# S5 recurrence as one chain per layer in a hybrid S5, RetNet and Hyena step

## The chip, the cores and the metric

The kernel runs on one core of one Trainium2 chip. The metric is the device time of one launch in microseconds; before the change it was 1736.06 us (median of three runs, 1731.86 to 1738.31). Five engines run side by side: PE multiplies matrices into PSUM, DVE, ACT and POOL work on elements, and SP issues most of the DMAs. Each engine takes its instructions in the order in which the program puts them.

## The reference

A trunk of four layers works on 128 context tokens and 256 latent tokens, 384 in all, with 1024 features. Layers 0 and 3 are bidirectional S5 layers, layer 1 is retention, layer 2 Hyena. An S5 layer projects its input to `u` and a gate, and drives one complex diagonal state of 64 dimensions for each of 64 groups of 16 features, in both directions:

```python
_, _, h_re, h_im = lax.associative_scan(combine, (a_re, a_im, bu_re, bu_im), axis=1)
y = (jnp.einsum('blgp,ghp->blgh', h_re, c_re) - jnp.einsum('blgp,ghp->blgh', h_im, c_im))
# in s5_branch, with y summed over both directions and the skip:
g = jax.nn.gelu(y)
y = g * jax.nn.sigmoid(g @ w_glu + b_glu)
out = (y * jax.nn.silu(gate)) @ w_out
```

The context starts from a zero state and returns its final states; the latent tokens start from states that are given (`h0`).

## The kernel before

Tokens are cut into chunks of eight: 16 chunks of context and 32 of latent tokens, 48 columns of states in all. Everything that can be done for all chunks at once is a matrix product; only the step from one chunk's state to the next is a recurrence, on DVE.

One S5 layer (`s5`, from line 692) runs in stages. The P stage follows a plan, a string of letters (`PLAN0` for layer 0, `PLAN1` for layer 3, lines 76 and 77). `U n` projects two blocks of features and sends them through DRAM into the layout `U` (`u_epi`, line 756). `A n` makes or loads the matrices PB up to number n; in layer 0 they are computed on DVE, POOL and PE (`gen_b1`, `gen_b2`), in layer 3 loaded. `P n` (`use_p`, line 733) multiplies them with `U`, transposes the product on PE, and ACT copies it into the states X (line 752). `T` runs a piece of background work, the modulation vectors of later layers (`mod_unit`, line 367). `R q` runs the recurrence of one half of the groups (`recur`, line 764): `R0` stands behind `P3`, `R1` at the plan's end.

X is held in two tiles (`Xs`, `NH = 2` halves of 32 groups). A tile has, for two directions and 32 groups, 49 places of one word each, so the neighbouring groups of one chunk lie 49 words apart. `recur` advances two chains, latent (31 steps) and context (16 steps), and each takes both directions in one instruction: 2 x 32 = 64 columns on 128 partitions. A step is five DVE instructions, lines 786 to 790: a shuffle that swaps real and imaginary lanes, X times A1, its addition to the next place, the shuffled state times A2, its addition. The context's last step goes into XF, which an ACT queue stores as the final states. The scratch tiles `sw` and `m1` are in the pool `tmp`, two buffers each.

Behind the plan comes the gate: `dense` (line 830) multiplies four slabs of weights of the input projection, eight units of 24 products, into PSUM tiles of the pool `pd`, which has three buffers. Each weight unit is split into a high and a low part (`unit`, line 156), the high on ACT, the low by a subtraction that in this stage is always POOL's (`sub_any`, line 144; `PSG = 3`); the split tiles have two buffers. `silu2` (line 529) ends a unit: tanh on ACT, then line 532 on DVE, which reads the PSUM tile and writes a block of `sgate`. `sgate` is the one tile of the pool `s5r`, [128, 8, 384] in f32.

The output stage (from line 854) is a loop over eight pairs of group blocks: line 874 multiplies U with a Toeplitz matrix, lines 875 and 876 add the states X times the matrices CP, forward and backward. Blocks 0 to 3 read the first half of X, 4 to 7 the second. In layer 0 some CP are computed on the way (`gen_c`, line 678): those of the first two blocks wholly on POOL (`CPG = 2`), others on DVE with one addition on POOL. GELU, the GLU projection and the output projection follow.

Pools are taken from a stack with a left and a right end and closed in the opposite order; those of `s5` have `reuse_waits="tile"`, so a tile waits for the users of earlier tiles on its own bytes. In a layer the left end holds, in this order, `s5h`, in layer 0 `s5t`, and then the P stage's pools: the ring of PB (`s5b`), `s5a` and in layer 0 `s5g`. They are closed at line 820, and `s5r` and `s5c` follow. The program's order on each engine is set by a scheduler that takes what stands earlier in the program first, among what it expects to be ready.

Of the kernel before, what the change touches and what calls it, by code (L numbers as in the profile page):

```python
# [10 lines left out]
F32 = mybir.dt.float32  # L11
# [15 lines left out]
NCH = T // Q  # L27
XP = NCH + 1
CC = NCTX // Q
# [4 lines left out]
SPLIT = True  # L34
RB = 7
NBC = 2
NH = 2
CPG = 2
RB1 = 10
CP1 = 6  # L40
# [32 lines left out]
GV = 7  # L73
LSQ = 0
FPB = (3, 6)
PLAN0 = "A7 U0 T1 U1 T1 P0 A9 T1 P1 A11 T1 U2 T1 P2 A13 T1 P3 A15 T1 R0 U3 T1 P4 T1 A16 P5 T1 T1 P6 P7 R1"
PLAN1 = "A10 U0 U1 P0 A12 P1 A13 U2 P2 A16 P3 R0 U3 P4 P5 P6 P7 R1"
SPL = (4, 6, 8, 10, 12, 14)
SPQ = "gpsimd"
KSE = "VG"  # L80
# [25 lines left out]
def hybrid_trunk(ctx: ExitStack, tc: tile.TileContext, I, O, dbg=None, layers=(0, 1, 2, 3)):  # L106
    nc = tc.nc
    V, S, G, TE = nc.vector, nc.scalar, nc.gpsimd, nc.tensor
# [5 lines left out]
    tmp = ctx.enter_context(tc.tile_pool(name="tmp", bufs=2))  # L114
# [577 lines left out]
    def s5(i, j, nxt, begun=lambda: None):  # L692
        def mk(st, name, bufs=1, **kw):
            return st.enter_context(tc.tile_pool(name=f"{name}_{i}", bufs=bufs, reuse_waits="tile", **kw))
# [3 lines left out]
        U = pool.tile([128, 8, 8 * NCH + 16], F32, name="U")  # L698
        XH = 64 // NH
        Xs = [pool.tile([128, 2 * XH, XP], F32, name=f"X{q}") for q in range(NH)]  # L700
        XFs = [pool.tile([128, 2, XH], F32, name=f"XF{q}") for q in range(NH)]
        hpool = mk(ep, "s5h")
# [13 lines left out]
                gates.popleft()()  # L716
        V.memset(U[:, :, 8 * NCH:], 0.0)
        eP = ExitStack()
        ring = mk(eP, "s5b", RB if j == 0 else RB1)
        ru = mk(eP, "s5a", 2)  # L720
        PBs = {}
# [42 lines left out]
        def recur(q):  # L764
            gs = slice(q * XH, (q + 1) * XH)
            A1, A2 = Av[:, 0, :, gs], Av[:, 1, :, gs]
            X, XF = Xs[q], XFs[q]
            Xb = X[:, 0, 0:1]
            V.tensor_copy(XF[:, 0], X[:, 0:XH, CC])
            V.tensor_copy(XF[:, 1], X[:, XH:2 * XH, 0])  # L770

            def view(c_f, c_b):
                return bass.AP(tensor=Xb.tensor, offset=Xb.offset + c_f,
                               ap=[Xb.ap[0], [XH * XP + c_b - c_f, 2], [XP, XH]])
            V.memset(view(0, CC), 0.0)
            V.tensor_copy(view(CC, NCH), h0.rearrange("p (d g) -> p d g", d=2)[:, :, gs])
            for k in range(NCH - CC - 1):
                for c0, n in ((CC, NCH - CC), (0, CC)):
                    if k >= n:
                        continue  # L780
                    c1 = c0 + n - 1
                    cur = view(c0 + k, c1 - k + 1)
                    dst = XF if k == n - 1 else view(c0 + k + 1, c1 - k)
                    sw = tmp.tile([128, 2, XH], F32, tag=f"sw{c0}{q}", name="sw")
                    m1 = tmp.tile([128, 2, XH], F32, tag=f"m1{c0}{q}", name="m1")
                    V.stream_shuffle(sw, cur, [(x + 16) % 32 for x in range(32)])  # L786
                    V.tensor_mul(m1, cur, A1)  # L787
                    V.tensor_add(dst, dst, m1)  # L788
                    V.tensor_mul(sw, sw, A2)  # L789
                    V.tensor_add(dst, dst, sw)  # L790
            nc.scalar.dma_start(O["ns5"][j].rearrange("p (d g) -> p d g", d=2)[:, :, gs], XF)

        nxp = 0
# [1 line left out]
        def ahead(n):  # L795
            nonlocal nxp
            while nxp < min(n, 16):
                get_p(nxp)
                nxp += 1
        if j == 0 and AI:  # L800
            with tc.issue_after(ADA[0]):
                ahead(AI)
        for op in (PLAN0, PLAN1)[j].split():
            n = int(op[1:])
            if op[0] == "A":
                ahead(n)
            elif op[0] == "U":
                if j == 0:
                    pool_share[0] = PS0 if n == 0 else 1
                firstmajor(i, weight(I["s5_w_in"][j, n]), h, u_epi, 2 * n)  # L810
                if n == 0:
                    begun()
            elif op[0] == "P":
                use_p(n)
            elif op[0] == "R":
                recur(n)
            else:
                tick(n)
        pool_share[0] = PSG
        eP.close()  # L820
        if j == 0:
            eT.close()
        rpool = mk(ep, "s5r")
        sgate = rpool.tile([128, NB, T], F32, name="sgate")

# [560 lines left out]
    def to3():  # L1386
        p = pool_of(e3, "x3", side="right")
        return Early(3, lambda: p.tile([128, T + 2], F32, tag="xb", name="xb", bufs=NB + EB3))
    s5(0, 0, to1)
    trace(0)  # L1390
    hp = pool_of(eh, "hp")
# [5 lines left out]
    e2.close()  # L1397
    eh.close()
    s5(3, 1, lambda: None, e3.close)
    trace(3)  # L1400
    rb, _ = rstd_bcast()
# [168 lines left out]
```

## Time and profile before

| | us |
|---|---|
| median of three runs | 1736.06 |
| lowest and highest run | 1731.86, 1738.31 |
| span of the profiled execution | 1732.9 |
| PE busy in it | 1576.3 (91%) |
| DVE busy in it | 1331.7 (77%) |
| POOL busy in it | 762.2 (44%) |
| ACT busy in it | 691.6 (40%) |

Layer 0 takes about the first 450 us of the span and layer 3 the last 300. The rows further down give the start of an instruction from the span's start, its duration in us, the engine, the line, what is written and read with shapes, and in brackets how long the engine was idle just before and what ended that. A group by line has a count, the busy time and the mean in ns. A row of a stretch has, for each engine, the busy time with the number of instructions, then the granted clock of PE (1.00 is its full level) and what the DMA engines did.

### The profile page before, as it was taken

To read this page: it belongs to the slowest core of one execution; us is meant where nothing else is said; L and a number is where in the kernel's file an instruction comes from. 1 tells how busy PE (TensorE), PEld (TensorE's weight loads), DVE (VectorE), ACT (ScalarE), POOL (GpSimd) and SP (SyncE) were. 2 spreads that over 40 slices of the span, in tenths; PEclk is the share of its full clock that TensorE was granted. 3 is DMA by queue.
4 is the path that set the end of the run, shared out by engine and by line. 5 is a ranking of instruction groups with operands and counts; after the bars stand their busy time and mean duration, and the time that the engine had idled before them with its cause. 6 is when DMAs were issued, how large, how long until landed. Compare 5 with 4: busy or idle time off the path is not lost. (4 is left out here: it accounts for less than half of the span.)

```text
span 1732.9 us, 27790 instructions
## 1 busy us (share of the span) xinstructions
PE 1576.3 (91%) x10370; PEld 1348.6 (78%) x10370; DVE 1331.7 (77%) x3064; ACT 691.6 (40%) x1275; POOL 762.2 (44%) x542
## 2 busy tenths in 40 slices
PE   5899856898899999999899999999999999986996
PEld 3565545787588888899879889888898797775996
DVE  8979999889886777747767788687687864399355
ACT  2434320343333343335354444454454543521343
POOL 2767352525274757532235545555566231230221
PEclk9799978999799999999989999999999999987998
DMA  8356655644655656543421222222222363755431
GB/s 339 110 184 221 185 124 151 211 178 146 219 163 169 203 183 211 180 137 129 142 87 65 95 95 74 95 71 73 95 89 74 122 240 114 212 166 174 132 121 62
DMA packets 103199, 253.02 MB, mean 146 GB/s; under 512 B 28023, under 2 KB 68056, under 8 KB 83480
## 3 DMA queue, kind: packets, MB, share of 16 engines
q1 hardware_dynamic: 80768, 200.12, 35.5%
q0 software_dynamic: 7376, 26.48, 4.5%
q10 hardware_dynamic: 14920, 24.65, 3.9%
q8 instruction: 82, 1.34, 0.3%
q14 instruction: 53, 0.43, 0.1%
HBM read 220.37 MB, written 30.83 MB: 145 GB/s over the span
## 5 line engine op out<-in xcount | busy, mean ns | idle before, releaser
L134 POOL TENSOR_TENSOR wl<-wr,wh 128x1024 fp32r<-128x1024 f32 (+2 forms) x101 | 248.9, 2465 | 342.6 <-ACT wh L162 320.1
L139 PE MATMUL psd<-hh,wh 128*128 128x384 f32 x880 | 308.8, 352 | 38.2 <-DVE sgate L532 33.2
L162 ACT CAST wh<-wr 128x1024 fp32r<-128x1024 f32 (+4 forms) x211 | 215.9, 1029 | 316.7 <-PE psd L139 221.2
L139 PE MATMUL psd<-hh,wl 128*128 128x384 f32 x880 | 308.0, 351 | 3.9 <-DVE wl L149 2.0
L139 PE MATMUL psd<-hl,wh 128*128 128x384 f32 x880 | 307.7, 350 | 0.4 <-DVE hl L470 0.2
L139 PEld LDWEIGHTS psd<-hh,wh 128*128 128x128 f32 x880 | 171.5, 195 | 49.3 <-issue 40.4
L149 DVE TENSOR_TENSOR wl<-wr,wh 128x1024 fp32r<-128x1024 f32 (+3 forms) x110 | 149.2, 1358 | 78.7 <-ACT wh L162 78.3
L139 PEld LDWEIGHTS psd<-hh,wl 128*128 128x128 f32 x880 | 170.6, 194 | 13.4 <-issue 6.4
L139 PEld LDWEIGHTS psd<-hl,wh 128*128 128x128 f32 x880 | 171.0, 194 | 10.2 <-issue 6.7
L134 POOL TENSOR_TENSOR BP<-BP,xt 128x512 f32<-128x512 f32 x64 | 97.6, 1528 | 82.3 <-DVE xt L630 49.2
L134 POOL TENSOR_TENSOR CP<-CP,xt 128x512 f32<-128x512 f32 x64 | 94.9, 1487 | 85.6 <-DVE xt L630 66.8
L139 PE MATMUL psd<-wh,hh 128*128 128x256 f32 x384 | 110.4, 292 | 1.5 <-ACT k L1070 1.5
L139 PE MATMUL psd<-wl,hh 128*128 128x256 f32 x384 | 110.0, 288 | 1.2 <-DVE wl L149 1.2
L139 PE MATMUL psd<-wh,hl 128*128 128x256 f32 x384 | 108.7, 285 | 0.0
L664 PE MATMUL psm<-BP,bc 128*32 128x128 f32 x512 | 76.0, 296 | 7.0 <-POOL BP L134 6.3
L139 PE MATMUL psd<-zb,wh 128*128 128x384 f32 x240 | 80.9, 338 | 0.0
L630 DVE TENSOR_TENSOR xt<-FI,bc 128x512 f32<-128x512 f32 x64 | 64.0, 1008 | 16.7 <-POOL BP L134 11.8
L139 PEld LDWEIGHTS psd<-wh,hh 128*128 128x128 f32 x384 | 73.8, 194 | 2.7 <-ACT k L1070 1.9
L139 PEld LDWEIGHTS psd<-wl,hh 128*128 128x128 f32 x384 | 74.3, 193 | 1.9 <-DVE wl L149 1.4
L139 PEld LDWEIGHTS psd<-wh,hl 128*128 128x128 f32 x384 | 74.3, 194 | 0.3 <-issue 0.2
L665 PE MATMUL psm<-ident,BP 128*128 128x128 f32 x256 | 69.7, 325 | 3.4 <-DVE kk L1013 2.0
L629 DVE TENSOR_TENSOR BP<-F,bc 128x512 f32<-128x512 f32 x64 | 57.9, 914 | 17.8 <-PE psm L665 15.5
(387 smaller groups left out, 4095.0 us busy)
## 6 DMA issues: line engine op xcount, KB each, us to landing
wr<-in_mod_w_dram SPq DMA_DIRECT2D x40, 1024.0 KB
wr<-in_hy_w_in_dram SPq DMA_DIRECT2D x32, 1024.0 KB
wr<-in_ret_w_in_dram SPq DMA_DIRECT2D x24, 1024.0 KB
wr<-in_s_w_in_dram SPq DMA_DIRECT2D x16, 1024.0 KB
wm<-in_mod_w_dram SPq DMA_DIRECT2D x8, 1024.0 KB
Tt<-scratch_kd_dram SPq DMA_DIRECT2D x128, 64.0 KB
wr<-in_s_w_glu_dram SPq DMA_DIRECT2D x8, 1024.0 KB
wr<-in_s_w_out_dram SPq DMA_DIRECT2D x8, 1024.0 KB
```

What stands on the lines that cost most here:

```text
L134: G.tensor_tensor(out, a, b, op=op)
L139: TE.matmul(out, lhs[a], rhs[b], start=start and i == 0, stop=stop and i == len(combos) - 1)
L149: V.tensor_sub(out, a, b)
L162: S.copy(hi, ap)
L629: eng.tensor_tensor(out, c1, x[:, 0].unsqueeze(2).to_broadcast([128, 4, 8, 16]), op=OP.mult)
L630: eng.tensor_tensor(t, c2, x[:, 1].unsqueeze(2).to_broadcast([128, 4, 8, 16]), op=OP.mult)
L664: TE.matmul(psk[32 * g:32 * g + 32, d * 128:(d + 1) * 128], xcf[:, g * 16:g * 16 + 32], bp, start=True, stop=True)
L665: TE.transpose(ps[:, g * 128:(g + 1) * 128], bp, ident)
```

## The change

The recurrence is run once a layer. `NH` becomes 1, so X is one tile of 64 groups, and the two halves' chains become one with 2 x 64 = 128 columns. The context no longer has steps of its own: it starts eight steps later (`LAG = 8`), and for 15 steps an access pattern with one more dimension takes the latent and the context place in the same instruction, 256 columns (`pair`); the last context step, into XF, stays alone. `R0` stands at the plan's end, behind `P7`, in both plans, and `R1` is gone. The scratch tiles `sw` and `m1` move from `tmp` to a pool of their own, `s5rr`, with one buffer each; it is opened ahead of the ring and closed behind it, before `s5r` is opened.

```diff
-NH = 2
+NH = 1
+LAG = 8
-PLAN0 = "A7 U0 T1 U1 T1 P0 A9 T1 P1 A11 T1 U2 T1 P2 A13 T1 P3 A15 T1 R0 U3 T1 P4 T1 A16 P5 T1 T1 P6 P7 R1"
-PLAN1 = "A10 U0 U1 P0 A12 P1 A13 U2 P2 A16 P3 R0 U3 P4 P5 P6 P7 R1"
+PLAN0 = "A7 U0 T1 U1 T1 P0 A9 T1 P1 A11 T1 U2 T1 P2 A13 T1 P3 A15 T1 U3 T1 P4 T1 A16 P5 T1 T1 P6 P7 R0"
+PLAN1 = "A10 U0 U1 P0 A12 P1 A13 U2 P2 A16 P3 U3 P4 P5 P6 P7 R0"
...
         eP = ExitStack()
+        eR = ExitStack()
+        rr = mk(eR, "s5rr")
         ring = mk(eP, "s5b", RB if j == 0 else RB1)
...
+            swap = [(x + 16) % 32 for x in range(32)]
+
+            def step(cur, dst, a1, a2, shape):
+                sw, m1 = (rr.tile(shape, F32, tag=f"{nm}{len(shape)}", name=nm) for nm in ("sw", "m1"))
+                V.stream_shuffle(sw, cur, swap)
+                V.tensor_mul(m1, cur, a1)
+                V.tensor_add(dst, dst, m1)
+                V.tensor_mul(sw, sw, a2)
+                V.tensor_add(dst, dst, sw)
+
+            def pair(k, s):
+                f, b = k - LAG + s, CC - (k - LAG) - s
+                return bass.AP(tensor=Xb.tensor, offset=Xb.offset + f,
+                               ap=[Xb.ap[0], [XH * XP + b - f, 2], [CC + LAG, 2], [XP, XH]])
+            wide = [a.unsqueeze(2).to_broadcast([128, 2, 2, XH]) for a in (A1, A2)]
             for k in range(NCH - CC - 1):
-                for c0, n in ((CC, NCH - CC), (0, CC)):
-                    if k >= n:
-                        continue
-                    c1 = c0 + n - 1
-                    cur = view(c0 + k, c1 - k + 1)
-                    dst = XF if k == n - 1 else view(c0 + k + 1, c1 - k)
-                    sw = tmp.tile([128, 2, XH], F32, tag=f"sw{c0}{q}", name="sw")
-                    m1 = tmp.tile([128, 2, XH], F32, tag=f"m1{c0}{q}", name="m1")
-                    V.stream_shuffle(sw, cur, [(x + 16) % 32 for x in range(32)])
-                    V.tensor_mul(m1, cur, A1)
-                    V.tensor_add(dst, dst, m1)
-                    V.tensor_mul(sw, sw, A2)
-                    V.tensor_add(dst, dst, sw)
+                if LAG <= k < LAG + CC - 1:
+                    step(pair(k, 0), pair(k, 1), *wide, [128, 2, 2, XH])
+                    continue
+                step(view(CC + k, NCH - k), view(CC + k + 1, NCH - k - 1), A1, A2, [128, 2, XH])
+                if k == LAG + CC - 1:
+                    step(view(CC - 1, 1), XF, A1, A2, [128, 2, XH])
...
         eP.close()
         if j == 0:
             eT.close()
+        eR.close()
```

## Rows read from the trace of the kernel before

**Rows 1.** Busy time by stretch: around the recurrence of layers 3 and 0.
```profile
1526.00:1594.00 68.00, 46.81 (x268) 40.61 (x266) 68.00 (x380) 13.37 (x23) 14.81 (x7) 0.80 0.59 170
...
202.00:250.00 48.00, 33.82 (x204) 29.88 (x203) 48.00 (x216) 11.08 (x19) 20.72 (x14) 0.86 0.50 135
250.00:272.00 22.00, 1.40 (x4) 0.80 (x4) 22.00 (x37) 1.33 (x2) 20.46 (x16) 0.56 0.26 58
```
**Rows 2.** Timeline of PE in layer 3's gate stage: first products of units.
```profile
1525.09 0.33 PE L139 MATMUL psd<-hh,wh 128*128 128x384 f32 x1
...
1529.25 0.33 PE L139 MATMUL psd<-hh,wh 128*128 128x384 f32 x1
...
1534.10 0.66 PE L139 MATMUL psd<-hh,wh 128*128 128x384 f32 x1 [4.34 <-DVE sgate L532]
1534.56 0.52 PE L139 MATMUL psd<-hl,wh 128*128 128x384 f32 x1
...
1539.36 0.48 PE L139 MATMUL psd<-hl,wh 128*128 128x384 f32 x1
```
**Rows 3.** Timeline of PE: where line 875 waited for X, both layers.
```profile
288.51 0.42 PE L875 MATMUL psm<-CP,X 128*48 128x128 f32 x2 [2.93 <-DVE X L790]
...
325.12 0.66 PE L875 MATMUL psm<-CP,X 128*48 128x128 f32 x2 [3.38 <-DVE X L790]
...
1594.40 0.66 PE L875 MATMUL psm<-CP,X 128*48 128x128 f32 x2 [4.86 <-DVE X L790]
```
**Rows 4.** Timeline of DVE: two chains side by side, one shuffle and its next.
```profile
1523.10 0.26 DVE L786 STREAM_SHUFFLE sw<-X 128x64 f32<-128x64 f32 x1
...
1524.78 0.25 DVE L786 STREAM_SHUFFLE sw<-X 128x64 f32<-128x64 f32 x1
```
**Rows 5.** Timeline of DVE: one chain alone, a whole step.
```profile
1598.15 0.26 DVE L786 STREAM_SHUFFLE sw<-X 128x64 f32<-128x64 f32 x1
1598.33 0.25 DVE L787 TENSOR_TENSOR m<-X,A 128x64 f32<-128x64 f32 x1
1598.50 0.21 DVE L789 TENSOR_TENSOR sw<-sw,A 128x64 f32<-128x64 f32 x1
1598.63 0.26 DVE L788 TENSOR_TENSOR X<-X,m 128x64 f32<-128x64 f32 x1
1598.93 0.27 DVE L790 TENSOR_TENSOR X<-X,sw 128x64 f32<-128x64 f32 x1
...
1599.24 0.26 DVE L786 STREAM_SHUFFLE sw<-X 128x64 f32<-128x64 f32 x1
```
**Rows 6.** DVE's groups by line and shape, whole span: widths and a strided copy.
```profile
L320 DVE TENSOR_TENSOR vs<-vs 128x128 f32<-128x128 f32 x4 | 1.1, 283 | 0.0
...
L176 DVE TENSOR_TENSOR zl<-zz,zh 128x384 fp32r<-128x384 f32 x16 | 8.8, 552 | 3.0 <-ACT zh L175 2.9
...
L1068 DVE STREAM_SHUFFLE rsw<-psd 128x256 f32<-128x256 f32 x16 | 7.2, 450 | 0.0
...
L770 DVE COPY XF<-X 128x32 f32<-128x32 f32 x4 | 0.7, 181 | 0.0
```
**Rows 7.** Timeline of ACT: the last copies of P7 into X.
```profile
201.31 1.01 ACT L752 COPY X<-psm 128x384 f32<-128x384 f32 x2 [3.15 <-PE psm L749]
...
1523.85 1.00 ACT L752 COPY X<-psm 128x384 f32<-128x384 f32 x2 [3.41 <-PE psm L749]
```
**Rows 8.** DVE's groups from 202 to 288.4 us: the recurrence's two-input operations.
```profile
L789 DVE TENSOR_TENSOR sw<-sw,A 128x64 f32<-128x64 f32 x59 | 22.9, 388 | 0.0
L787 DVE TENSOR_TENSOR m<-X,A 128x64 f32<-128x64 f32 x57 | 22.3, 391 | 0.0
L788 DVE TENSOR_TENSOR X<-X,m 128x64 f32<-128x64 f32 x57 | 22.3, 391 | 0.0
L790 DVE TENSOR_TENSOR X<-X,sw 128x64 f32<-128x64 f32 x57 | 20.1, 409 | 0.0
```
**Rows 9.** POOL's groups from 1525.2 to 1594.4 us.
```profile
L134 POOL TENSOR_TENSOR wl<-wr,wh 128x1024 fp32r<-128x1024 f32 x6 | 14.6, 2432 | 23.8 <-ACT wh L162 23.7
```

## The prediction

> **What bounds the kernel now.** I read the busy time by stage first, then PE's timeline, then DVE's own timeline, and last what POOL does beside it. In the stage after the last state projection of layer 3, from 1526 to 1594 us, DVE is busy 68.00 us of 68.00 and PE 46.81 [rows 1]: the recurrence is the bound there. PE has only the gate projection left and stands behind DVE, since a PSUM tile of the gate comes free only when DVE has run line 532 on it: 4.34 us at 1534.10 [rows 2]. Then PE waits for X: line 875, the first product that reads the states, begins at 1594.40 in layer 3 and at 288.51 in layer 0, both released by line 790 [rows 3]. In layer 0 a second wait of 3.38 us stands at 325.12, for the second half of the groups [rows 3]. So in both layers the end of the recurrence sets when the output stage begins. Layer 0 is worse off: from 250 to 272 us PE works 1.40 us of 22 while POOL is busy 20.46 [rows 1].
>
> **What the change removes.** 47 steps by two halves and two layers are 188 steps, of five instructions each. Two chains side by side take 1.68 us for two steps, from shuffle to shuffle [rows 4], 0.84 each; 94 steps a layer are 79 us of DVE. Where one chain runs alone, a step takes 1.09 us, as 0.18 + 0.17 + 0.13 + 0.30 + 0.31 from start to start [rows 5]: the last two carry about 0.12 us more, because each needs the result of the instruction just ahead of it. The new recurrence is always one chain.
>
> **What it adds.** A layer has 16 + 1 steps on 128 columns and 15 on 256. A contiguous two-input operation takes 283 ns at 128 columns and 552 at 384, thus 1.05 ns a column [rows 6]; back to 64 that gives 216, what line 789 takes (0.21), and lines 787, 788 and 790, which read or write X at a stride of 49 words, take 0.25 to 0.27 [rows 5]. The excess of some 45 ns is either a price of each strided column, 0.7 ns, or a fee per instruction. I take the first: the 32-column copy out of X takes 181 ns [rows 6], where 216 less 32 columns (34) plus a fee of 45 would be 227 and the price by column 204. The trace has no wide strided operation, so this is a bound from both sides and not shown. [...] The shuffle grows from 0.26 us at 64 columns to 0.450 at 256 [rows 5, 6], 1.0 ns a column from a contiguous source; between that and 1.75 I take 1.4. So a step on 128 columns is 1.09 + 3 x 0.112 + 0.067 + 0.09 = 1.58 us and one on 256 is 1.09 + 3 x 0.336 + 0.202 + 0.27 = 2.57. 17 x 1.58 + 15 x 2.57 = 65.4 us a layer: a third of the instructions, but only 14 us less DVE time.
>
> **What it moves.** The first chain began after P3 and ran beside P4 to P7; now nothing begins until P7's copies into X end, at 202.32 in layer 0 and 1524.85 in layer 3 [rows 7]. The four set-up instructions cost about 0.6 us. DVE's work in the P stage goes away, but PE is full there, so I take no gain; at most 3 us. Of queues, only the store of XF on ACT moves; it leaves once, near the end, behind gate work that is then done.
>
> **POOL's holds.** Two-input DVE operations stand still while POOL runs one: between 202 and 288.4 us the four lines average 391, 391, 388 and 409 ns [rows 8] against 0.25, 0.26, 0.21 and 0.27 [rows 5], which is 8.0 + 7.5 + 10.5 + 7.9 = 34 us, 0.82 of the 41.2 us that POOL was busy from 202 to 272 [rows 1]. I price a hold at 0.82 of POOL's time; the ends are 0.6 (a wider operation gets more done between two holds) and 1.0.
>
> **The wait that it adds.** `s5rr` is opened ahead of the ring and closed behind it, and `s5r` is the next pool opened on that side. Pools are stacked, so `s5r` begins on the byte where `s5rr` began: `sgate`, 12 KB a partition, covers the 3 KB of `sw` and `m1`. With `reuse_waits="tile"` a tile waits for all users of earlier tiles on its bytes; here the last is the recurrence's last addition. Before, `sw` and `m1` lay in `tmp` and `sgate` stood on ring tiles, dead after P7. So every line 532 must follow the whole recurrence on DVE. Behind it are queued: three finished PSUM tiles of the gate, all that `pd` has, and thus PE's gate units 4 to 8. They had run beside the recurrence; now they run after it. One unit is 24 products from 1525.09 to 1529.25, 4.16 us at full clock [rows 2], five are 20.8. After that wait PE's products take 0.32 us each against 0.173, fifteen from 1534.56 to 1539.36, 2.4 us lost with the first two [rows 2]; the granted clock of the stretch is 0.80 [rows 1]. With 0.5 us for line 532 (552 ns at 384 columns, [rows 6]) PE reaches the output stage's work 23.7 us after the recurrence ends, whichever of the two it takes first.
>
> **Layer 3.** 1524.85 + 0.6 + 65.4. Of POOL's six subtractions in that stretch (2.43 us each, [rows 9]) only the splits of three units still find a buffer ahead of the end: 3 x 2.43 x 0.82 = 6.0. The recurrence ends at 1596.9, the output stage is at 1620.6 against 1594.40: 26 us later.
>
> **Layer 0.** POOL's 24 operations of `gen_c` stay beside the recurrence (41.2 less six subtractions of 2.4 leaves 27) with three subtractions, 34.2 x 0.82 = 28. 202.32 + 0.6 + 65.4 + 28 = 296.3, and with 23.7 it is 320.0 against 288.51, 31.5 later. The wait of 3.38 us at 325.12 goes, since all groups now end together: 28.
>
> **Sum.** 54 us on the span of 1732.9, that is 1787. The runs' median of 1736.06 is 3.2 above this execution's span, so I forecast 1790.
>
> **Rivals.**
> *The gate isn't held back*: `sgate` waits by the bytes really shared or lies elsewhere, and the eight line 532 slip into the chain's gaps. For it: I read the overlap from the code, and no row shows such a wait. Then 8 x 0.47 us join the recurrence, and all six subtractions: layer 3 ends at 1524.85 + 0.6 + 65.4 + 12.0 + 3.8 = 1606.7, 12 later; layer 0 at 202.32 + 0.6 + 65.4 + 34 + 3.8 = 306.1, 18 less 3.4 later. 1736 + 26 = 1762.
> *The stride is a fee per instruction*, the gate held: steps of 1.09 + 5 x 0.067 = 1.43 and 1.09 + 5 x 0.202 = 2.10 give 55.7 a layer, 19 less in all: 1771. The copy of 181 ns speaks against it.
> *Not slower: a step costs the same whatever its width*, as if only the count of instructions mattered. 32 x 1.09 = 35 us a layer, 30.5 less in each: layer 3 is 4 us ahead of before and layer 0 about 2.5, 1736 - 7 = 1729. It decides from about 35 us a layer, a mean of 0.22 us an instruction. The rows of 283 and 552 ns speak against it; what speaks for it is that no wide strided row exists.
>
> **How the numbers follow.** About half a per cent, 8.7 us, is what a measurement of this kernel can tell from no change: same is 1727.4 to 1744.7. The held gate 0.66, its own range 1772 to 1806 (holds at 0.6 or 1.0 of POOL's time are 15 us apart over both layers, the shuffle's slope 4, products of the gate that PE moves ahead a few). The gate not held 0.16, of which 0.03 below 1744.7. The fee 0.08. Flat steps 0.10, half of it below 1727.4. Slower 0.66 + 0.13 + 0.08 = 0.87, same 0.03 + 0.05 = 0.08, faster 0.05. From 1755 to 1806 lie nearly all of the held gate and the fee and most of the second case, about 0.8.
>
> **What would show it.** Right: lines 786 to 790 come 32 times a layer each; wide operations on X take 0.59 to 0.63 us (0.37 to 0.39 on 128 columns); no line 532 between the first and the last shuffle of a layer; PE idle for most of the recurrence and then five gate units before or among the output stage. Wrong: line 532 among the steps, 256-column operations of 0.45 us, a first line 875 ahead of 1594 us in layer 3, or a P stage that ends much earlier.

## The result and the profile after

The changed kernel takes 1791.7 us (median of four runs, 1788.35 to 1796.04) against 1737.0 for the kernel before beside it: a ratio of 1.0314, 95% interval 1.0289 to 1.0339. The forecast was 1790. The profiled execution has a span of 1788.8 us, 55.9 longer than the one before.

The page's head comes first, engine by engine (share of the span, instructions).

```profile
PE 1566.9 (88%) x10370; PEld 1343.1 (75%) x10370; DVE 1279.1 (72%) x2312; ACT 690.7 (39%) x1275; POOL 765.1 (43%) x542
```

DVE has 52.6 us less work than before (1331.7) and PE about the same, and yet the span is longer: PE waits more. The busy time by stretch tells where (layer 3's recurrence, the time just behind it, the later part of layer 0's recurrence; columns as in rows 1).

```profile
1551.00:1623.00 72.00, 14.18 (x79) 12.61 (x77) 69.68 (x188) 6.42 (x11) 7.84 (x4) 0.58 0.30 78
1625.00:1655.00 30.00, 30.00 (x197) 27.02 (x199) 3.34 (x7) 6.26 (x10) 8.30 (x5) 0.97 0.37 123
250.00:290.00 40.00, 0.00 (x0) 0.00 (x0) 38.96 (x104) 0.00 (x0) 4.71 (x4) 0.50 0.03 8
```

Before, PE was busy 46.81 us of 68 beside layer 3's recurrence [rows 1]; now it is 14.18 of 72 beside the recurrence and 30.00 of 30 behind it. From 250 to 290 us it does nothing at all, at a granted clock of 0.50. PE's timeline shows the waits that answer to rows 3, and what follows the second one.

```profile
291.34 0.63 PE L887 MATMUL psm<-CP,X 128*48 128x128 f32 x2 [58.67 <-DVE X L788]
...
1624.05 0.66 PE L887 MATMUL psm<-CP,X 128*48 128x128 f32 x2 [50.21 <-DVE X L788]
...
1628.01 0.44 PE L140 MATMUL psd<-hh,wh 128*128 128x384 f32 x1
```

One wait of 58.67 and one of 50.21 us have taken the place of 2.93, 3.38 and 4.86 [rows 3], and four microseconds after the second, line 140 is running: gate units, which before ran ahead of it [rows 2]. DVE's timeline has the reason: the first writes of `sgate` in layer 0, then the end of layer 3's recurrence with a step on 256 columns, a step on 128 and the first writes of `sgate` there.

```profile
291.23 1.48 DVE L533 SCALAR_TENSOR_TENSOR sgate<-silu,psd 128x384 f32<-128x384 f32 x3
...
1586.08 0.60 DVE L784 STREAM_SHUFFLE sw<-X 128x256 f32<-128x256 f32 x1
1586.59 0.59 DVE L785 TENSOR_TENSOR m<-X,A 128x256 f32<-128x256 f32 x1
1587.10 0.42 DVE L787 TENSOR_TENSOR sw<-sw,A 128x256 f32<-128x256 f32 x1
1587.43 0.61 DVE L786 TENSOR_TENSOR X<-X,m 128x256 f32<-128x256 f32 x1
1588.07 0.61 DVE L788 TENSOR_TENSOR X<-X,sw 128x256 f32<-128x256 f32 x1
...
1588.73 0.60 DVE L784 STREAM_SHUFFLE sw<-X 128x256 f32<-128x256 f32 x1
...
1615.95 0.38 DVE L784 STREAM_SHUFFLE sw<-X 128x128 f32<-128x128 f32 x1
1616.24 0.37 DVE L785 TENSOR_TENSOR m<-X,A 128x128 f32<-128x128 f32 x1
1616.53 0.28 DVE L787 TENSOR_TENSOR sw<-sw,A 128x128 f32<-128x128 f32 x1
1616.73 0.38 DVE L786 TENSOR_TENSOR X<-X,m 128x128 f32<-128x128 f32 x1
1617.14 0.39 DVE L788 TENSOR_TENSOR X<-X,sw 128x128 f32<-128x128 f32 x1
...
1617.57 0.38 DVE L784 STREAM_SHUFFLE sw<-X 128x128 f32<-128x128 f32 x1
...
1623.61 0.39 DVE L788 TENSOR_TENSOR X<-X,sw 128x128 f32<-128x128 f32 x1
1624.09 1.48 DVE L533 SCALAR_TENSOR_TENSOR sgate<-silu,psd 128x384 f32<-128x384 f32 x3
```

The first writes of `sgate` are three of line 533 in a row, in layer 3 0.1 us behind the last addition of the last step. In both layers none of the eight writes of `sgate` stands between the first and the last shuffle; in the kernel before all eight do. The three are the three full PSUM tiles that the prediction spoke of. A step from shuffle to shuffle takes 1.62 us on 128 columns and 2.65 on 256.

How the 55.9 us are spread is read from the start of the same instructions in both traces. Layer 1's first product of queries and keys comes at 493.1 and 523.3 us: up to there the change costs 30.2, which I count to layer 0. Layer 2's last product (line 497 here, 496 before) starts 25.8 later, so layers 1 and 2 give 4.4 back, and the last copy into X in layer 3 starts 24.7 later. Layer 3's first product with X is 29.6 later, its last 55.6, the end 55.9: layer 3 costs 30.1, of which its P stage (up to that copy) gives 1.1 back and the rest takes 31.2.

### The profile page after: what moved, and what is told of

Read it like the earlier page. It is cut to its first block, busy times and chain, and to the rows that moved or that the text cites. A ratio compares the mean times of both kernels' runs of the same rounds, so it can differ in the third digit from the quotient of the medians.

```text
span 1788.8 us, 27046 instructions
## 1 busy us (share of the span) xinstructions
PE 1566.9 (88%) x10370; PEld 1343.1 (75%) x10370; DVE 1279.1 (72%) x2312; ACT 690.7 (39%) x1275; POOL 765.1 (43%) x542
## 3 DMA queue, kind: packets, MB, share of 16 engines
q8 instruction: 82, 1.34, 0.3%
## 5 line engine op out<-in xcount | busy, mean ns | idle before, releaser
L140 PE MATMUL psd<-hl,wh 128*128 128x384 f32 x880 | 303.7, 345 | 4.5 <-DVE hl L471 4.4
L140 PE MATMUL psd<-hh,wh 128*128 128x384 f32 x880 | 303.8, 346 | 3.3 <-ACT wh L163 3.3
L140 PE MATMUL psd<-hh,wl 128*128 128x384 f32 x880 | 303.6, 346 | 0.7 <-DVE wl L150 0.7
L140 PEld LDWEIGHTS psd<-hh,wh 128*128 128x128 f32 x880 | 167.8, 191 | 13.5 <-issue 6.0
L887 PE MATMUL psm<-CP,X 128*48 128x128 f32 x256 | 50.7, 282 | 108.9 <-DVE X L788 108.9
L887 PEld LDWEIGHTS psm<-CP,X 128*48 128x48 f32 x256 | 30.1, 127 | 112.7 <-issue 62.0
```

The lines of the kernel that those rows point to most:

```text
L140: TE.matmul(out, lhs[a], rhs[b], start=start and i == 0, stop=stop and i == len(combos) - 1)
L887: TE.matmul(o48, Xs[gg // XH][:, gg % XH, 0:48], CP[r][:, 0, g].rearrange("p a b -> p (a b)"), start=False, stop=False)
```

## The experiments

All kernels beside each other, in the order of the text. "Chain" is the time from the start of the last copy into X (line 752 before) to the first product with X (line 875 before), "output" from there to the start of the last one (line 876 before), from the view of each line; both for layers 0 and 3. Ratios are to the kernel before on the same chip (medians from 1736.0 to 1737.3), with 95% intervals.

| kernel | us | ratio | chain 0 | output 0 | chain 3 | output 3 |
|---|---|---|---|---|---|---|
| before | 1737.0 | | 86.7 | 62.0 | 70.0 | 54.8 |
| after | 1791.7 | 1.0314 (1.0289 to 1.0339) | 95.6 | 83.7 | 74.9 | 80.8 |
| e1_free | 1755.2 | 1.011 (1.0075 to 1.0145) | 104.8 | 56.7 | 85.8 | 55.8 |
| e2_lock | 1778.9 | 1.0231 (1.0208 to 1.0255) | 76.6 | 92.6 | 59.7 | 87.2 |
| e3_halves | 1732.7 | 0.9968 (0.9953 to 0.9984) | 62.3 | 89.1 | 61.7 | 58.6 |
| e8_late | 1769.9 | 1.0187 (1.0163 to 1.0211) | 112.6 | 60.7 | 88.4 | 55.9 |
| e10_unmerged | 1770.7 | 1.0202 (1.0177 to 1.0227) | 111.7 | 58.0 | 91.4 | 56.2 |
| e4_contig | 1735.1 | 0.9982 (0.9967 to 0.9997) | 92.9 | 58.0 | 68.3 | 55.4 |
| e5_halves_contig | 1713.0 | 0.9867 (0.9848 to 0.9886) | 58.9 | 79.7 | 47.9 | 60.0 |
| e9_contig3 | 1715.1 | 0.9877 (0.9862 to 0.9892) | 60.3 | 89.1 | 48.0 | 55.1 |
| e6_nopool | 1778.9 | 1.0241 (1.0226 to 1.0257) | 79.0 | 84.3 | 74.9 | 81.7 |

### Is it the wait of `sgate`?

**e1_free**, the changed kernel without the overlap:

```diff
-        eR = ExitStack()
-        rr = mk(eR, "s5rr")
...
-                sw, m1 = (rr.tile(shape, F32, tag=f"{nm}{len(shape)}", name=nm) for nm in ("sw", "m1"))
+                sw, m1 = (tmp.tile(shape, F32, tag=f"{nm}{len(shape)}", name=nm, bufs=1) for nm in ("sw", "m1"))
...
-        eR.close()
```

> The changed kernel with one thing undone: the scratch tiles sw and m1 lie in the pool tmp again (one buffer each), so sgate shares no byte with them. Theory (the wait of sgate on the recurrence's scratch is what costs most): the eight lines that write sgate slip between the steps, the gate units of the matrix engine run beside the recurrence again, and the stage from the first product with X to the last falls from 80.8 us in layer 3 and 83.2 in layer 0 (changed kernel) to 55 to 60. The recurrence gets 8 x 0.47 us and three more subtractions of POOL, 3 x 2.43 x 0.82, thus about 10 us longer in each layer. 1791.7 - 2 x 25 + 2 x 10 = about 1762. Rival (one chain that is always ready keeps VectorE full, and the gate would come behind it in any case): no line that writes sgate among the steps, 1785 to 1795.

It took 1755.2 us, 36.5 less than the changed kernel. DVE's timeline in layer 3 has the writes of `sgate` among the steps again (this kernel's line numbers are two to three lower):

```profile
1536.35 0.29 DVE L785 TENSOR_TENSOR sw<-sw,A 128x128 f32<-128x128 f32 x1
1536.55 2.60 DVE L784 TENSOR_TENSOR X<-X,m 128x128 f32<-128x128 f32 x1
1538.99 0.54 DVE L533 SCALAR_TENSOR_TENSOR sgate<-silu,psd 128x384 f32<-128x384 f32 x1
1539.46 0.37 DVE L786 TENSOR_TENSOR X<-X,sw 128x128 f32<-128x128 f32 x1
```

Line 533 even falls into the gap between two dependent additions, and in both layers all eight writes of `sgate` stand among the steps. The output stages of layers 3 and 0 shrink to 55.8 and 56.7 us as the theory said, and the chains grow by 10.9 and 9.2. The rival, that a chain which is always ready would keep the gate behind it anyway, is out.

**e2_lock**, the kernel before with that overlap alone:

```diff
+        eR = ExitStack()
+        rr = mk(eR, "s5rr", 2)
         ring = mk(eP, "s5b", RB if j == 0 else RB1)
...
-                    sw = tmp.tile([128, 2, XH], F32, tag=f"sw{c0}{q}", name="sw")
-                    m1 = tmp.tile([128, 2, XH], F32, tag=f"m1{c0}{q}", name="m1")
+                    sw = rr.tile([128, 2, XH], F32, tag=f"sw{c0}{q}", name="sw")
+                    m1 = rr.tile([128, 2, XH], F32, tag=f"m1{c0}{q}", name="m1")
...
+        eR.close()
         rpool = mk(ep, "s5r")
```

> The kernel before with that wait alone: its scratch tiles (two buffers) in a pool that is opened ahead of the ring of PB and closed behind it, so that sgate falls on their bytes. Four chains, two halves, as before. Theory: all lines that write sgate come behind both halves' recurrence, and the matrix engine's gate units 4 to 8 (five x 4.16 us) with the half-clock ramp move behind it; since the first half of the output stage can start without the gate, part of the 27 us of that half covers the second half's recurrence: layer 0 about 17 us later, layer 3 about 15, 1737 + 32 = 1769 (1755 to 1784). Rival (the wait is harmless): 1737, or up to 10 less since the steps are no longer interrupted.

1778.9 us, 42 more than before, within the range but above the 32. DVE again ends the recurrence and then writes three tiles at once:

```profile
1619.45 0.27 DVE L792 TENSOR_TENSOR X<-X,sw 128x64 f32<-128x64 f32 x1
1619.82 1.49 DVE L532 SCALAR_TENSOR_TENSOR sgate<-silu,psd 128x384 f32<-128x384 f32 x3
```

So the wait alone costs 42 us in the kernel with four chains, and by e1 36.5 of the 55 in the changed one. I had let the second half's chain hide part of the gate units. The output stage of layer 3 is 32.4 us longer than before, though its chain is 10.3 shorter: PE is busy 83.33 of the 87.40 us from 1607.6 on, so the gate units had nothing to hide behind.

### Which part of the rest is the cost?

**e3_halves** keeps the merged step but in two halves, with the plans of before and the scratch of e1:

```diff
-NH = 1
+NH = 2
...
-PLAN1 = "A10 U0 U1 P0 A12 P1 A13 U2 P2 A16 P3 U3 P4 P5 P6 P7 R0"
+PLAN1 = "A10 U0 U1 P0 A12 P1 A13 U2 P2 A16 P3 R0 U3 P4 P5 P6 P7 R1"
```

> The merged step, but in two halves of 32 groups with the plans of before (R0 behind P3, R1 at the end), scratch in tmp. A half has 17 steps on 64 columns and 15 on 128. Theory (what the merged step loses is the gap of a lone chain, about 0.25 us a step, and the start behind P7; width costs by the column): the two halves fill each other's gaps, steps side by side cost 0.84 us at 64 columns and about 1.4 at 128, so 34 x 0.84 + 30 x 1.4 = 70.6 us a layer against 79 before, and the first half again starts in the P stage: 7 us less per layer than the kernel before, 1723 (1712 to 1737). Rival (merging gains nothing since the time is by the column alone): 1735 to 1742.

**e8_late** is e3 with the first half made to wait: in both plans `R0` stands beside `R1` behind `P7`, both halves' XF copies come first, and the start values of a half are `0 * XFs[1]`, plus `h0`, so they need P7. Of the edit, the start values:

```diff
...
-            V.memset(view(0, CC), 0.0)
-            V.tensor_copy(view(CC, NCH), h0.rearrange("p (d g) -> p d g", d=2)[:, :, gs])
+            V.tensor_scalar(view(0, CC), XFs[1], 0.0, None, op0=OP.mult)
+            V.scalar_tensor_tensor(view(CC, NCH), XFs[1], 0.0, h0.rearrange("p (d g) -> p d g", d=2)[:, :, gs],
+                                   op0=OP.mult, op1=OP.add)
```

> e3 with one thing undone: both halves start together behind the last copy into X, since the first half's start values are made from a tile that the last block fills (0 times it, added). Theory (the early start of the first half is worth its DVE time in the P stage, 8 x 1.09 + 5 x 1.58 = 16.6 us in layer 3, and the two halves then end together): from the last copy into X to the first product with X, layer 3 goes from 61.7 us to 80 to 86, about what the single chain of e1 took (85.8), and the time to 1748 to 1756. Rival (the start is of no worth, since the second half ends last in either case): 1730 to 1738.

e3 took 1732.7 us: faster than before, but by 4, not 14. Layer 3 gives what was expected, 7.4 us from layer 2's last product to the end (P stage 2.8 shorter, chain 61.7 against 70.0, output 3.8 longer). Layer 0 gives nothing: its chain is 24.4 us shorter and its output stage 27.1 longer, and layer 1's first product of queries and keys comes 7.8 later, of which layers 1 and 2 give 4.8 back. Before e3's first product with X in layer 3, PE waits 3.78 us. In e8, PE's timeline has 26.23:

```profile
1631.80 0.66 PE L886 MATMUL psm<-CP,X 128*48 128x128 f32 x2 [26.23 <-DVE X L788]
```

e8 is 37.2 us slower than e3. The theory's sign held and its chain came close (80 to 86 us, measured 88.4), but its total of some 20 counted layer 3 only, and layer 0 loses nearly as much (173.3 us for chain and output against 151.4; layer 3 144.3 against 120.3). The rival, that the early start is of no worth, is out. What it is worth is two things at once, DVE work in the P stage and a half that ends ahead of the other; I did not part them.

**e10_unmerged** is the kernel before with `NH = 1` and the plans of the changed kernel: one tile, late start, but latent and context in instructions of their own.

```diff
-NH = 2
+NH = 1
...
-PLAN1 = "A10 U0 U1 P0 A12 P1 A13 U2 P2 A16 P3 R0 U3 P4 P5 P6 P7 R1"
+PLAN1 = "A10 U0 U1 P0 A12 P1 A13 U2 P2 A16 P3 U3 P4 P5 P6 P7 R0"
```

> The kernel before with one part of the change alone: one tile X of all 64 groups (128 columns), the recurrence behind P7, but latent and context chain still in instructions of their own, scratch in tmp. Set beside e1, which differs from it only in that both chains share their instructions. Theory (the time of a step is by the column, and two chains side by side fill the gap that a lone one leaves): 16 pairs at 2 x 1.40 us and 15 lone latent steps at 1.62 are 69.1 us a layer against 67.3 in e1, so it is within 4 us of e1's 1755 (1753 to 1762): merging context and latent saves 75 instructions a layer and nearly no time. Rival (an instruction saved is worth a fixed cost, some 0.15 us each): 75 x 0.15 = 11 us a layer above e1, 1772 to 1782.

My number was wrong: 1770.7 us, 15.5 above e1 and just below the rival's range. Its reason is not the rival's, though. The timeline of DVE in layer 3 shows steps that follow each other alone, a whole one first, and further on a pair of steps side by side, from its first shuffle to the next step's:

```profile
1564.47 0.37 DVE L786 STREAM_SHUFFLE sw<-X 128x128 f32<-128x128 f32 x1
1564.76 0.36 DVE L787 TENSOR_TENSOR m<-X,A 128x128 f32<-128x128 f32 x1
1565.04 0.28 DVE L789 TENSOR_TENSOR sw<-sw,A 128x128 f32<-128x128 f32 x1
1565.24 0.37 DVE L788 TENSOR_TENSOR X<-X,m 128x128 f32<-128x128 f32 x1
1565.65 0.39 DVE L790 TENSOR_TENSOR X<-X,sw 128x128 f32<-128x128 f32 x1
...
1566.08 0.38 DVE L786 STREAM_SHUFFLE sw<-X 128x128 f32<-128x128 f32 x1
...
1589.84 0.39 DVE L786 STREAM_SHUFFLE sw<-X 128x128 f32<-128x128 f32 x1
...
1592.59 0.37 DVE L786 STREAM_SHUFFLE sw<-X 128x128 f32<-128x128 f32 x1
```

A step alone takes 1.61 us, as a lone one of 128 columns does in the merged kernel (1.62), and a pair side by side 2.75, against 2.65 for a merged step. The five instructions that merging saves are thus worth 0.10 us where a pair runs side by side, not the rival's 0.75. But in both layers only 9 of the 16 pairs run side by side, and 29 steps run alone where I had expected 15: the order of DVE left the other pairs apart, and two lone steps are 3.2 us. Layer 3's recurrence took 89.7 us from its first shuffle to its last addition, e1's 84.1. Less e1's 16.8 us of holds and gate writes (84.1 less 17 x 1.62 and 15 x 2.65; POOL's subtractions take 14.7 us here and 14.8 there) that is 73 us, and 9 pairs with 29 lone steps make some 72. So merging saves some 6 us a layer, most of it by closing the gaps of lone steps and little by saving instructions. The chains of the two layers make 12.5 of the 15.5 us; the rest I did not follow up.

### What a column costs

**e4_contig** is e1 with another layout of X, chunk by chunk:

```diff
-        Xs = [pool.tile([128, 2 * XH, XP], F32, name=f"X{q}") for q in range(NH)]
+        Xs = [pool.tile([128, 2, XP, XH], F32, name=f"X{q}") for q in range(NH)]
...
-                               ap=[Xb.ap[0], [XH * XP + c_b - c_f, 2], [XP, XH]])
+                               ap=[Xb.ap[0], [(XP + c_b - c_f) * XH, 2], [1, XH]])
...
-                    TE.matmul(o48, Xs[gg // XH][:, gg % XH, 0:48], CP[r][:, 0, g].rearrange("p a b -> p (a b)"), start=False, stop=False)
+                    TE.matmul(o48, Xs[gg // XH][:, 0, 0:48, gg % XH], CP[r][:, 0, g].rearrange("p a b -> p (a b)"), start=False, stop=False)
```

> e1 with X laid out chunk by chunk, so that the 64 groups of one chunk and direction lie side by side in place of 49 words apart; the copies of ScalarE into X and the loads of X on the matrix engine now hop instead. Theory (the stride is paid per column): shuffle aside, the three instructions of a step that touch X fall from 0.38 to 0.28 us at 128 columns and from 0.60 to 0.42 at 256, the shuffle likewise, so 17 x 4 x 0.10 + 15 x 4 x 0.18 = 17.6 us less a layer if the shuffle follows, 13 if not: e1 minus 26 to 35. Rival 1 (a fee per instruction of 45 ns): 32 x 3 x 0.045 = 4.3 us a layer, e1 minus 9. Rival 2 (the hop is paid again elsewhere): the 16 copies a layer into X grow from 0.485 us, or the loads of X from 0.12, and the time is that of e1 or above.

The same step on 256 columns in DVE's timeline of e4:

```profile
1569.42 0.45 DVE L782 STREAM_SHUFFLE sw<-X 128x256 f32<-128x256 f32 x1
1569.77 0.41 DVE L783 TENSOR_TENSOR m<-X,A 128x256 f32<-128x256 f32 x1
1570.09 0.42 DVE L785 TENSOR_TENSOR sw<-sw,A 128x256 f32<-128x256 f32 x1
1570.42 0.42 DVE L784 TENSOR_TENSOR X<-X,m 128x256 f32<-128x256 f32 x1
1570.88 0.42 DVE L786 TENSOR_TENSOR X<-X,sw 128x256 f32<-128x256 f32 x1
...
1571.35 0.44 DVE L782 STREAM_SHUFFLE sw<-X 128x256 f32<-128x256 f32 x1
```

1.93 us instead of 2.65. Layer 3's chain falls by 17.5 us where 17.6 was expected (with the shuffle), so the stride is paid by the column, and the fee is out. In all e4 gains 20 us, not 26 to 35: layer 0 gives nothing, as the second rival had it for both layers. The copies into X, which hop now, are dearer, as ACT's groups from 1480 to 1530 us show (mean 852 ns, 488 before):

```profile
L753 ACT COPY X<-psm 128x384 f32<-128x384 f32 x16 | 12.0, 852 | 12.9 <-PE psm L750 12.9
```

and in layer 0 DVE waits 17.4 us for the last of them, which starts 12.4 us later than in e1 (2.6 of it are there at layer 0's first product with U already; the dearer copies are 16 x 0.36 = 5.8, and the rest is not traced); chain and output together are 10.6 us shorter there and end 1.8 later. The loads of X on PE grow too, from 0.123 to 0.157 us, but lie beside the products.

**e5_halves_contig** joins e3 and e4; **e9_contig3** has e4's layout in layer 3 alone (strides chosen by layer, otherwise e5).

> The two halves of e3 with the chunk-by-chunk layout of e4 in both layers. Theory (the stride is paid by the column, and in layer 3 the recurrence is the bound, in layer 0 the matrices that are generated): from the last copy into X to the first product with X, layer 3 falls from 61.7 us (e3) by 26 x 4 x 0.09 + 22 x 4 x 0.04 = about 12, less 1.5 us for the slower copies; layer 0 gains nothing, since its P stage grows as in e4 (0.36 us more for each of 16 copies into X, and DVE waits for them). 1732.7 - 11 = 1722 (1715 to 1727). Rival (with halves the gate projection on the matrix engine is the bound in layer 3 already): 1730 to 1736.

> e5 with the new layout in layer 3 alone; layer 0 has the layout of e3. Theory as for e5: in layer 3 about 11 us less than e3; layer 0 as in e3, so its P stage is not longer: 1721 (1715 to 1726), at most 3 us under e5. Rival (the layout is worth the same in layer 0, where the recurrence would be the bound too): about 6 to 10 us above e5.

e5 is the fastest of all: 1713.0 us, 1.3% below the kernel before, and below its own range of 1715 to 1727. Layer 3's chain is 13.8 us shorter than e3's, where some 10.5 were forecast (12 less 1.5). Layer 0 gained 5 us, where I had allowed nothing: its last product with X starts at 348.8 us against 354.2. e9 has the same chain in layer 3 (48.0) and stands 2 us above e5, less than the intervals tell apart. The rival was near the truth in layer 0, where e5 is 5 us ahead; but e5 loses as much again in layer 3, whose chain and output together take 107.9 us against 103.1 in e9. PE's views of the two output stages show the 4.9 us: a wait of 2.5 for the DMA of a tile `Tt` (line 858), and 2.4 more of PE's busy time for the same products (57.64 against 55.20 us) at a mean granted clock of 0.97 against 1.00. Whether the layout brings that about is not shown.

### What POOL's work costs the recurrence

**e6_nopool** loads stored matrices in place of the first two blocks' CP in layer 0:

```diff
...
-                if j == 0 and 2 * m + r not in SPL:
+                if j == 0 and 2 * m + r not in SPL and m >= CPG:
...
-                    (CQ if j else nc.sync).dma_start(c.rearrange("p d g e c -> p (d g e c)"), I["cpd"][2 * m + r])
+                    (CQ if j else nc.sync).dma_start(c.rearrange("p d g e c -> p (d g e c)"), I["cpd"][2 * m + r if m >= CPG or j else 4])
```

> The changed kernel, but in layer 0 the matrices CP of the first two blocks are not generated on POOL: other, already stored ones are loaded in their place, so this kernel leaves that part of the computation out. Theory (a two-input operation of VectorE stands still while POOL works; 0.82 of POOL's time, 27 us of it here): the recurrence of layer 0 falls from 94.3 us by 22, to about 72, close to layer 3's 74; the time falls by about 20, to 1772 (1767 to 1777), the loads being off the path. Rival (layer 0's recurrence is longer for another reason, the generation on VectorE between the steps or the matrix engine's work): 90 us or more, 1786 to 1795.

POOL's groups in the changed kernel from 196.5 to 291.2 us, and then in e6 from 201.5 to 280 us:

```profile
L135 POOL TENSOR_TENSOR CP<-CP,xt 128x512 f32<-128x512 f32 x10 | 14.6, 1477 | 21.9 <-DVE xt L631 21.9
L631 POOL TENSOR_TENSOR xt<-BI,xc 128x512 f32<-128x512 f32 x8 | 10.7, 1339 | 0.0
L630 POOL TENSOR_TENSOR CP<-B,xc 128x512 f32<-128x512 f32 x8 | 10.5, 1319 | 12.2 <-DMA xc<-in_s5bc_dram 12.2
L135 POOL TENSOR_TENSOR wl<-wr,wh 128x1024 fp32r<-128x1024 f32 x3 | 7.5, 2503 | 11.4 <-ACT wh L163 9.8 <-PE psn L380 1.6
```

```profile
L135 POOL TENSOR_TENSOR wl<-wr,wh 128x1024 fp32r<-128x1024 f32 x3 | 7.3, 2427 | 20.1 <-ACT wh L163 18.5 <-PE psn L380 1.6
L135 POOL TENSOR_TENSOR CP<-CP,xt 128x512 f32<-128x512 f32 x2 | 4.2, 2110 | 30.0 <-DVE xt L631 30.0
```

31.8 us less of POOL (43.3 to 11.5) shorten layer 0's chain by 16.6 us, from 95.6 to 79.0: 0.52 of POOL's time and not 0.82. The total falls by 12.8, to 1778.9, between the ranges of the theory and of the rival. The last copy into X starts 5.2 us later in e6, of which 2.7 are there at layer 0's first product with U already; that is no part of the edit that I could follow.

## Why the prediction was right, point by point

The steps can be priced along a path of kernels of which each differs from the next in one main thing: before, e3, e8, e1, after. Another path would share the sum out differently; on its own, in e2, the last row costs 42.

| step | us |
|---|---|
| latent and context merged, in halves (before to e3) | -4.3 |
| both halves start behind P7 and end together (e3 to e8) | +37.2 |
| one chain over all groups in place of two (e8 to e1) | -14.7 |
| `sgate` on the scratch's bytes (e1 to after) | +36.5 |

**The bound.** Right. The output stage follows line 788 in both layers, by waits of 58.67 and 50.21 us.

**The counts and the price of a step.** 32 steps a layer came, 17 on 128 columns and 15 on 256. 128 columns were to take 1.58 us and took 1.62; 256 were to take 2.57 and took 2.65. The operations on X take 0.37 to 0.39 and 0.59 to 0.61 us, as named. The term that was too small is the shuffle's: I took 1.4 ns a column, and 0.60 us at 256 against 0.26 at 64 [rows 5] is 1.8, so it pays the stride like the others. A layer's steps cost 17 x 1.62 + 15 x 2.65 = 67.3 us, not 65.4. The rivals that needed another price, the fee (0.46 us at 256 columns) and the flat step, are refuted by these rows and by e4. At the 49 words of X a product that reads it takes 1.72 ns a column, (0.59 - 0.37) us over 128 more columns; the prediction had 1.75, which is 1.05 contiguous and 0.7 for the stride.

**The start.** "At most 3 us" of gain in the P stage was wrong in layer 0: the last copy starts at 195.7 us instead of 201.8, 6 us earlier. Of that 1.3 are there at layer 0's first product with U already, and the other 4.9 fit the steps that DVE no longer runs there: from e3 to e8, where these steps leave the P stage too, the same stretch falls by 4.6. In layer 3 the stage is 1.1 us shorter. The late start itself was in the sum and is its largest hidden term, +37 by e8; the prediction never priced it, since it worked from the absolute time of P7.

**The wait.** The mechanism is shown from both sides, by e1, which takes the wait away, and by e2, which puts it into the kernel before. Of the 23.7 us behind the recurrence, 20.8 were gate units, and they are there: the groups of PE's products from 1624.05 to 1705.1 us hold three times 40 of line 140 on `psd`, five units, which the kernel before has not in its output stage.

```profile
L140 PE MATMUL psd<-hh,wl 128*128 128x384 f32 x40 | 13.7, 343 | 0.0
L140 PE MATMUL psd<-hh,wh 128*128 128x384 f32 x40 | 13.6, 340 | 0.0
L140 PE MATMUL psd<-hl,wh 128*128 128x384 f32 x40 | 13.4, 335 | 0.0
L380 PE MATMUL psn<-wr,sgc 128*32 128x256 f32 x64 | 4.3, 385 | 0.0
```

The 2.4 us of half clock were mis-sized: in layer 3 the kernel before entered its output stage at the low clock too, with the same 0.66 us for the first two products [rows 3] (granted clock 0.50 from 1594.40 to 1595.60, and 0.50 in the changed kernel from 1624.05 to 1625.20), and the stage's mean granted clock is 0.97 before and 0.98 after, so they are no difference. In their place stands what I had not counted, 64 products of background work (line 380), 4.3 us, whose results DVE must also take out and which had been done by then before. The output stage of layer 3 is 26.0 us longer, 20.8 + 4.3 and a rest of 0.9; that of layer 0 is 21.7 longer, though the second wait of 3.38 [rows 3] is gone.

**POOL's holds.** In layer 3 the forecast was 6.0 us, and three operations were held, 2.64, 2.19 and 1.98 us beyond their 0.38, 0.28 and 0.39:

```profile
1551.17 3.02 DVE L786 TENSOR_TENSOR X<-X,m 128x128 f32<-128x128 f32 x1
...
1555.28 2.47 DVE L787 TENSOR_TENSOR sw<-sw,A 128x128 f32<-128x128 f32 x1
...
1559.73 2.37 DVE L788 TENSOR_TENSOR X<-X,sw 128x128 f32<-128x128 f32 x1
```

6.8 us for 7.3 us of POOL, 0.93 of it. In layer 0 the 28 us came out right by luck, from two errors. DVE's 94.3 us from 196.9 to 291.2 are 67.3 of steps, 5.0 of `gen_c` on DVE itself (six operations that the prediction left out), and the remaining 22, of 43.3 us of POOL: a hold of 0.51, below the 0.6 that I gave as the lower end, on more POOL time than the 34.2 that I had. Part of that time is new: POOL's lines of `gen_c` took 1.32 to 1.48 us an operation on average, where the same lines took 1.11 to 1.26 in the kernel before, so POOL ran slower too. e6 gives 0.52 by another way.

**The sums.** Layer 3's output stage started 4.9 us later beside its own last copy where 2.5 were expected (1596.9 against 1594.4), its output stage grew by 26.0 and not 23.7, and layer 3 in all cost 30.1, not 26. Layer 0 cost 30.2, not 28: it started 6 us earlier than thought, and lost 5.7 more between its last product with X and layer 1's first of queries and keys. Most of these 5.7 are PE's own: about as many products (755, and 756 before) kept it busy 129.5 us against 125.1, at a mean granted clock of 0.90 against 0.92. What lowered the clock there stays open. Layers 1 and 2 gave 4.4 back. That 55.9 came so near to 54 is luck: the terms are further off than their sum. The second case, the gate not held, was put at 1762; e1 is that kernel and took 1755.2, so the rest of the change costs 18 us and not 26, mainly because layer 0's chain ends at 299.4 us and not at 306.1.

## What to carry to other kernels

When scratch moves to a pool of its own, ask what is next allocated on its bytes and who stands behind that tile's first write: here it made 36.5 of 55 us, with as many products on PE and as many instructions on DVE as without it. The chains of dependent steps here were priced by columns and gaps, hardly by instructions (five fewer were worth 0.10 us where a pair ran side by side): merging closes the gaps of a lone chain (most of some 6 us a layer), but one big chain that must wait for the last input and feeds its first reader only at its very end lost more than that (e1 took 22.5 us more than e3); keep a part that starts and ends early. And let the engine with the longest chain have the contiguous side of a layout, and pay the hop where there is slack: e5 took 19.7 us less than e3.

## What the runs showed of the hardware that I had not expected

A shuffle pays the stride like a two-input operation (0.60 us for 256 columns at 49 words, 0.45 contiguous), and an addition that reads and writes X at the stride costs hardly more (0.61) than a product that only reads it so (0.59). ACT pays a hop on its writes: 384 columns took 0.49 us and 0.85 when each word lay 64 words on (e4). No shuffle here was held by POOL (all 64 of the changed kernel took 0.36 to 0.61 us): six on 256 columns ran wholly beside POOL's operations in layer 0 and took 0.60 to 0.61 us, as without them. In layer 0 of the changed kernel POOL runs an operation from 227.13 to 228.47 us (line 631, 1.34 us); the shuffle at 226.20, beside POOL's operation ahead of it, takes its usual 0.61, and the product at 227.48 ends only behind POOL's operation:

```profile
226.20 0.61 DVE L784 STREAM_SHUFFLE sw<-X 128x256 f32<-128x256 f32 x1
226.72 0.83 DVE L785 TENSOR_TENSOR m<-X,A 128x256 f32<-128x256 f32 x1
227.48 1.27 DVE L787 TENSOR_TENSOR sw<-sw,A 128x256 f32<-128x256 f32 x1
```

The six shuffles use 3.6 of POOL's 43.3 us. They are one reason why the steps of layer 0 lost a smaller share of POOL's time (0.51) than those of layer 3 (0.93), whose three holds fell on 128 columns. POOL's operations are also longer there, 2.4 us each where most in layer 0 take 1.3 to 1.5; which of the two counts for more is not shown.
